# A hybrid layer of five token mixers: the attention's value products four key tiles at a time, its maxima transposed with 128 columns, its denominators after the next unit's products

## The chip, the cores and the metric

The kernel runs on one core of one Trainium2 chip. The metric is the device time of one execution in microseconds (us). Of the kernel before, three runs are given, and their median is the time that counts.

## What is computed

One layer over 2048 tokens of width 1024: a norm, one input projection to 4652 columns, five mixers of 256 columns each (spatial gate, forgetting attention "FoX", mLSTM, RWKV-7, attention to a memory of 256 rows), gates, and one output projection with the residual. The change touches the two attentions only:

```python
def forgetting_attention(q, k, v, f_logit, q_g, k_g):      # 4 heads of 64
    q = rms_norm(to_heads(q), q_g)
    k = rms_norm(to_heads(k), k_g)
    v = to_heads(v)
    big_f = jnp.cumsum(jax.nn.log_sigmoid(f_logit), axis=1)
    ...
        s = jnp.einsum("bthd,bshd->bhts", qb, k) * scale
        s = s + fb[..., :, None] - big_f[..., None, :]
        s = jnp.where(k_pos[None, :] <= q_pos[:, None], s, -jnp.inf)
        p = jax.nn.softmax(s, axis=-1)
        return jnp.einsum("bhts,bshd->bthd", p, v)
...
def memory_attention(q, mem_n, w_kv, q_g, k_g):            # 256 keys, no mask
    ...
    p = jax.nn.softmax(s, axis=-1)
    return jnp.einsum("bhtm,bmhd->bthd", p, v)
```

## The kernel before

The kernel goes through three phases of input projections and one of output projections. Each projection is done in three products of high and low parts on TensorE (L266, L288, L300, L314, L878). Beside them run "lanes": generators that issue a stage of other work at each `tick()`, which comes every few projection products. All engines take their instructions in the order in which this interleaving issues them.

The attentions are one lane, `fox`, with 1.815 steps to a tick (1.0 to a tick during the output projection). Their work is cut into 32 units of 512 queries of one head: 16 of FoX with 4, 8, 12 and 16 key tiles of 128 keys (`nkt`), and 16 of the memory with 2. The order is 15 units of FoX, 4 of the memory, the last of FoX, 12 of the memory. `Attention.run` (L931) takes a unit `n` through `average`, in `nkt + 3` steps, and meanwhile issues `load` and `maxima` of unit `n + 2` and `finish` of unit `n - 1`; the loops at L838, L844 and L848 call steps with no projection work between them.

- `load` (L978): loads keys and queries, rounds them to high parts and takes low parts. The tile `qb` (68 rows) holds the high parts of the queries and four more rows; two of those are set to one at L1010 in every unit.
- `maxima` (L1029): scores with queries on partitions (L1025, L1027), reduced by VectorE (L1039); the row maxima go to a tile `mm` of 4 columns per 128 queries (two constant ones from L1062, and a high and a low part by `split4`, L1018 and L1019), are transposed by four products against an identity matrix (L1067) and copied to the last rows of `qb` (L1068).
- `weights` (L1070): two or three products (L1080, L1082 for the mask, L1083) to one of two PSUM banks `p2`, and an exponential on ScalarE (L1085).
- `rest` (L1088): GpSimd adds the exponentials of all key tiles (L1097, L1099).
- `product` (L1101): the values weighted, two key tiles at a time. Even tiles go to the left 64 columns of the array, odd ones to the right 64, so a pair runs side by side. There is one PSUM bank `acc`, and the first product of the next unit waits until `finish` has read it.
- `finish` (L1123): copies one half of `acc` (L1137), adds the other (L1139), multiplies by the gate (L1141); the denominators are four products of 32 columns each (L1146), copied by ScalarE (L1148).
- `quotient` (L1151): a chain of DMAs through DRAM in ten stages, one at each call of `Attention.end`: denominators out (L1156), two stages later back in another shape (L1160), two later the reciprocal and out (L1163, L1164), two later in to 64 partitions (L1168), two later the product on VectorE (L1171), one later out to the gated branches (L1173). Each step of `run` calls `end` once; at its start, `finish` calls `end` again and again while more than one quotient is under way (L1131).

The output projection of 512 queries begins when the quotients of these queries are issued to the end (L848).

Of the kernel before, what the change touches and what calls it, by code (L numbers as in the profile page):

```python
# [35 lines left out]
# 256-column blocks of the input projection, by the first column of each  # L36
# [8 lines left out]
# narrow columns: (first column, width, first row of the transposed block)  # L45
NARROW = [(3340, 16, 0), (2564, 4, 16), (2568, 4, 20), (1536, 4, 24), (3868, 16, 32)]

# columns of the packed per-partition parameters
# [15 lines left out]
class Lane:  # L64
    """a queue of work that is emitted a stage at a time, between the parts of the projections"""
# [19 lines left out]
class Crowd:  # L85
    """short pieces of work that go on side by side, a stage at a time; a stage that has read a projection for the last
    time gives FREE"""
# [9 lines left out]
    def add(self, g, kind=None, most=2):  # L97
        """kind: what takes the same buffers, of which there are so many"""
        while sum(k == kind for _, k in self.all) >= most and kind:
            self.tick()  # L100
        if self.step(g):
            self.all.append((g, kind))
# [8 lines left out]
    def then(self, g):  # L111
        """g, behind all that is under way now"""
        wait = list(self.all)
        while any(x in self.all for x in wait):
            yield
        yield from g
# [3 lines left out]
def body(ctx: ExitStack, tc, x, xT, mem, memT, wp, wkv, wout, pv, wa, sguT, sgub, out, dbg=None):  # L120
# [26 lines left out]
    def rsqrt(t):  # L147
        """in place, of up to 16 positive columns: half of the exponent, negated, then Newton's steps to the last bit"""
# [8 lines left out]
    # parameters that stand behind a tanh, a doubled SiLU or a doubled GELU  # L157
# [47 lines left out]
    def load_w(parts, src, ncol=256):  # L205
        """hi and lo parts of a block of 256 columns, 2 row blocks to a tile"""
# [42 lines left out]
    def W(n):  # L249
        """the weights of this block; those of the next one are sent for"""  # L250
# [9 lines left out]
    def proj_T(wt, m, hts):  # L260
        """[128 columns, 512 tokens] of the projection"""
# [10 lines left out]
    def proj_narrow(wt, hts):  # L272
        """64 columns: the products of their hi parts above those of the lo parts"""
# [8 lines left out]
    def proj_T2(wt, hts, then=None):  # L282
        """both halves of a block at once: for the last use of the row blocks"""
# [10 lines left out]
    def proj_tok2(wt, hts, then=None, ntile=4):  # L294
        """all tokens at once"""
# [11 lines left out]
    def proj_tok(wt, hts, i):  # L307
        """[128 tokens, 256 columns] of the projection, twice: tokens i * 128 on and the next 128"""
# [11 lines left out]
    def split_h(hts, src_of, g, N):  # L320
        """hi and lo parts of (normalised x) * g, one tile for each of the 8 row blocks"""
# [16 lines left out]
    def send(*a):  # L338
        """the next row blocks are sent for"""
# [10 lines left out]
    def rstd(pool, tags, src, ntile):  # L350
        """1/rms of each token, tokens on partitions; tags: of the buffers for half of the columns of 128 tokens"""
# [20 lines left out]
    def rstd_rows(pool, tags, rb, src, ntile):  # L372
        """1/rms of each token, as a row over all partitions"""
# [4 lines left out]
    def over(ss, rb, ntile):  # L378
        """from tokens on partitions to a row over all partitions"""
# [5 lines left out]
    def gate(pt, o, then=lambda: None, free=FREE):  # L385
        """twice the SiLU"""
# [6 lines left out]
    def head_norm(pt, n, eps, pool=None):  # L393
        """1/rms over the 64 columns of each head; n columns on 128 tokens"""
# [13 lines left out]
    def qk_post(y, scale, d):  # L408
        """normalised over each head, scaled, transposed: to d"""
# [30 lines left out]
    def tok_cols(wt, hts, i, d):  # L440
        """tokens on partitions, to DRAM"""
# [10 lines left out]
    with ExitStack() as c1:  # L452
# [12 lines left out]
        def first(hts):  # L465
            """the first tokens: the norm is put to what comes out, so that the products need not wait for it"""
# [58 lines left out]
        for q in range(NQ):  # L525
# [8 lines left out]
            def shifted(pt, j, then):  # L534
                """token shift of a block of 128 columns"""
# [92 lines left out]
    def conv(pt, j, o):  # L628
        """causal convolution over 4 tokens, then twice the SiLU"""
# [13 lines left out]
    def group_B(q):  # L643
        """queries, keys, values and gates of FoX"""
# [11 lines left out]
    def group_M(q, then=None):  # L656
        """queries and gates of the attention to the memory"""
# [7 lines left out]
    for q in range(NQ):  # L665
# [32 lines left out]
    def gelu2(pt, o):  # L698
        """twice the tanh GELU"""
# [33 lines left out]
    # keys and values of the memory; its norm is put to what comes out  # L733
# [27 lines left out]
    for q in (NQ - 1, 0, 1, 2):  # L761
# [4 lines left out]
        if q == NQ - 1:  # L766
# [12 lines left out]
            # the first quarter of the attention to the memory goes before the last part of FoX  # L779
# [5 lines left out]
            # masked transposed weights and bias rows of the spatial gate  # L785
# [37 lines left out]
    def load_wo():  # L823
        """hi and lo parts of 128 rows of one half of the columns"""
# [22 lines left out]
    for q in range(NQ):  # L847
# [4 lines left out]
        def load_m(j):  # L852
            """256 tokens of the gated branches"""
# [34 lines left out]
class Attention:  # L888
    """what the attentions share"""
# [7 lines left out]
    def open(self):  # L897
# [8 lines left out]
        # 0 where the key may be seen, with keys on partitions, then with queries there  # L906
# [12 lines left out]
        self.minus = fp.tile([P, 1, 1], F32, bufs=1, name="minus")  # L919
        G.memset(self.minus, -1.0)  # L920
        self.two = fp.tile([P, 32], F32, bufs=1, name="two")
        G.memset(self.two, 2.0)

# [38 lines left out]
class Unit:  # L962
# [145 lines left out]
    def average(self):  # L1108
        self.acc = self.att.bank("acc")
        late, pair = deque(), []  # L1110
        for kt in range(self.nkt + 3):
# [4 lines left out]
            if kt > 2:  # L1116
                pair.append(late.popleft())
                if len(pair) == 2:
                    self.product(pair)
                    pair = []  # L1120
# [631 lines left out]
```

## Time and profile before

| | us |
|---|---|
| three runs | 1748.2, 1752.41, 1760.76 |
| median | 1752.41 |
| profiled execution, first to last instruction | 1753.3 |
| TensorE busy in it | 1654.2 |
| VectorE busy | 1197.5 |
| ScalarE busy | 880.9 |
| GpSimd busy | 302.8 |

PE is TensorE's products, PEld its weight loads, DVE VectorE, ACT ScalarE, POOL GpSimd, SP the queue that issues most DMAs. Matmul records overlap, as products are pipelined: what a product costs the engine is read from the start of one line to the start of the next. A product of plain f32 leaves two records, one of the rounded type (fp32r, as L266, L1067, L1080 and L1083) one. "Idle" in brackets is time in which the engine did nothing, and after the arrow is what ended it. The attentions' units lie between about 989 and 1602 us from the start of the span; the last 150 us are output projection alone.

### The profile page before, as it was taken

To read this page: it belongs to the slowest core of one execution; us is meant where nothing else is said; L and a number is where in the kernel's file an instruction comes from. 1 tells how busy PE (TensorE), PEld (TensorE's weight loads), DVE (VectorE), ACT (ScalarE), POOL (GpSimd) and SP (SyncE) were. 2 spreads that over 40 slices of the span, in tenths; PEclk is the share of its full clock that TensorE was granted. 3 is DMA by queue.
4 is the path that set the end of the run, shared out by engine and by line. 5 is a ranking of instruction groups with operands and counts; after the bars stand their busy time and mean duration, and the time that the engine had idled before them with its cause. 6 is when DMAs were issued, how large, how long until landed. Compare 5 with 4: busy or idle time off the path is not lost.

```text
span 1753.3 us, 31654 instructions
## 1 busy us (share of the span) xinstructions
PE 1654.2 (94%) x11306; PEld 1282.0 (73%) x11306; DVE 1197.5 (68%) x2990; ACT 880.9 (50%) x1895; POOL 302.8 (17%) x356
## 2 busy tenths in 40 slices
PE   8889999899999999999999899998999998899999
PEld 6667777787978888787888666756655665577887
DVE  7688684775978579587766986878576777642220
ACT  5566654544464545446455765565555657531110
POOL 5020000010101001010000244354444142000000
PEclk9999999899999999999999999999999999899999
DMA  6878554443544354344435554434324335754431
GB/s 207 259 236 245 179 173 101 137 118 94 144 130 122 104 149 124 85 123 129 119 88 167 148 152 112 109 95 121 85 78 111 106 77 162 184 142 122 129 125 59
DMA packets 200151, 234.36 MB, mean 134 GB/s; under 512 B 75016, under 2 KB 107336, under 8 KB 199992
## 3 DMA queue, kind: packets, MB, share of 16 engines
q1 hardware_dynamic: 185144, 218.69, 43.6%
q10 hardware_dynamic: 14848, 13.64, 2.6%
q8 instruction: 89, 1.46, 0.4%
q14 instruction: 70, 0.57, 0.1%
HBM read 180.44 MB, written 51.81 MB: 132 GB/s over the span
## 4 chain that ended last, share of the span: by engine, by line
PE 58%; DVE 18%; DMA 14%; ACT 6%; issue 4%; SPq 1%; POOL 0%; ACTq 0%; DVEq 0%; POOLq 0%
PE pj L266 12%; PE pj L878 12%; PE pj L314 11%; DMA wraw<-in_wp 4%; PE pj L288 3%; PE acc L1106 3%; DMA xr<-hbd 3%; DVE wt L224 2%; PE wk L1025 2%; DMA ao<-dn 2%; PE p L1080 2%; PE p L1083 1%; PE pj L300 1%; DMA xr<-in_xT 1%; DVE rq L153 1%
## 5 line engine op out<-in xcount | busy, mean ns | idle before, releaser
L266 PE MATMUL pj<-ht,wt 128*128 128x512 f32 x1632 | 427.6, 404 | 6.0 <-ACT ht L328 4.2
L266 PEld LDWEIGHTS pj<-ht,wt 128*128 128x128 f32 x1632 | 298.3, 190 | 83.8 <-issue 9.8
L314 PE MATMUL pj<-wt,ht 128*128 128x256 f32 x2400 | 337.3, 292 | 6.9 <-ACT ht L328 2.4
L314 PEld LDWEIGHTS pj<-wt,ht 128*128 128x128 f32 x2400 | 308.1, 195 | 24.6 <-issue 5.8
L224 DVE TENSOR_TENSOR wt<-wraw,wt 128x512 fp32r<-128x512 f32 (+1 forms) x312 | 220.3, 709 | 94.0 <-ACT wt L221 92.5
L221 ACT CAST wt<-wraw 128x512 fp32r<-128x512 f32 (+1 forms) x312 | 184.7, 600 | 148.8 <-DMA wraw<-in_wp 103.1
L878 PE MATMUL pj<-wo,mt 128*128 128x512 f32 x960 | 232.7, 399 | 2.5 <-ACT wo L829 2.3
L878 PEld LDWEIGHTS pj<-wo,mt 128*128 128x128 f32 x960 | 180.3, 190 | 53.7 <-issue 6.9
L1099 POOL TENSOR_TENSOR es<-es,pe 128x512 f32<-128x512 f32 (+3 forms) x128 | 155.2, 1212 | 107.9 <-ACT pe L1085 99.2
L288 PE MATMUL pj<-ht,wt 128*128 128x512 f32 x480 | 135.5, 421 | 13.3 <-ACT wt L221 12.4
L1085 ACT ACTIVATE pe<-p 128x512 f32<-128x512 f32 x192 | 100.7, 541 | 67.9 <-PE p L1083 65.4
L1039 DVE TENSOR_REDUCE mx<-wk 128x1 f32<-128x512 f32 (+3 forms) x192 | 112.5, 615 | 16.6 <-PE wk L1025 11.2
L288 PEld LDWEIGHTS pj<-ht,wt 128*128 128x128 f32 x480 | 91.2, 199 | 38.1 <-ACT wt L221 12.8
L1106 PE MATMUL acc<-pe,v 128*64 128x512 f32 (+3 forms) x384 | 106.9, 580 | 5.9 <-DVE at L1139 5.1
L1097 POOL TENSOR_TENSOR es<-pe 128x512 f32<-128x512 f32 (+1 forms) x32 | 43.3, 1353 | 249.3 <-ACT pe L1085 207.1
L329 DVE SCALAR_TENSOR_TENSOR ht<-xr,pvt,ht 128x512 fp32r<-128x512 f32 (+1 forms) x88 | 68.6, 786 | 24.8 <-ACT ht L328 24.1
L858 ACT CAST mt<-mr 128x256 fp32r<-128x256 f32 x80 | 31.9, 406 | 102.7 <-DVE xr L882 45.9
L1080 PE MATMUL p<-qa,kb 128*128 128x512 f32 x192 | 76.9, 400 | 6.7 <-ACT pe L1085 6.7
L328 ACT ACTIVATE ht<-xr,pvt 128x512 fp32r<-128x512 f32 (+1 forms) x88 | 61.0, 701 | 42.5 <-DMA xr<-hbd 26.7
L882 DVE TENSOR_TENSOR xr<-pj,xr 128x512 f32<-128x512 f32 x32 | 22.0, 688 | 85.6 <-PE pj L878 85.5
L1025 PEld LDWEIGHTS wk<-ka,qb 66*128 66x128 f32 x224 | 40.4, 191 | 49.5 <-issue 17.7
L1025 PE MATMUL wk<-ka,qb 66*128 66x512 f32 (+3 forms) x224 | 72.5, 378 | 4.2 <-DVE mx L1039 1.4
(332 smaller groups left out, 2471.5 us busy)
## 6 DMA issues: line engine op xcount, KB each, us to landing
wraw<-in_wp SPq DMA_DIRECT2D x288, 256.0 KB
xr<-hbd SPq DMA_DIRECT2D x56, 256.0 KB
mr<-mix SPq DMA_DIRECT2D x80, 128.0 KB
xr<-in_x SPq DMA_DIRECT2D x32, 256.0 KB
out<-xr ACTq DMA_DIRECT2D x32, 256.0 KB
xt<-in_x SPq DMA_DIRECT2D x24, 256.0 KB
xr<-in_xT SPq DMA_DIRECT2D x24, 256.0 KB
hbd<-xr SPq DMA_DIRECT2D x24, 256.0 KB
```

Of the source, the lines that this page charges most:

```text
L221: A.copy(wt[:, :, 0, :ncol], raw[:, :, :ncol])
L224: V.tensor_tensor(lo, raw[:, :, :ncol], wt[:, :, 0, :ncol].bitcast(F32), op=ALU.subtract)
L266: T.matmul(pt, wt[k // 2][:, k % 2, a, m * P:(m + 1) * P], hts[k][:, b, :], start=n == 0, stop=n == 3 * KT - 1)
L288: T.matmul(pts[m], wt[k // 2][:, k % 2, a, m * P:(m + 1) * P], hts[k][:, b, :], start=k + n == 0, stop=k == KT - 1 and n == 2)
L314: T.matmul(pt[:, ii * 256:ii * 256 + 256], hts[k][:, a, (i + ii) * P:(i + ii + 1) * P], wt[k // 2][:, k % 2, b, :], start=n == 0, stop=n = ...
L878: T.matmul(po, mts[i // 2, k][:, a, i % 2 * P:(i % 2 + 1) * P], wo[e * NK + k][:, b], start=n == 0, stop=n == 3 * NK - 1)
L1025: T.matmul(p1, self.qb[0:66, i * P:(i + 1) * P], self.k[kk][0][0:66, :w], start=True, stop=True, skip_group_check=diag)
L1039: V.tensor_reduce(*late.pop(), axis=AX.X, op=ALU.max)
L1080: T.matmul(p2[:, f:], kb[:, ks], self.qa[:, f:], start=True, stop=False)
L1085: A.activation(e[:, f:], p2[:, f:], AF.Exp)
L1099: G.tensor_tensor(self.sum[:, f:], self.sum[:, f:], e[:, f:], op=ALU.add)
L1106: self.att.nc.tensor.matmul(self.acc[64 * i:64 * i + 64, f:], self.v[:, kt], e[:, f:], start=kt < 2, stop=True, skip_group_check=True)
```

## The change

Five edits, all in `Attention` and `Unit`; in addition comments and docstrings of the whole file are dropped.

1. `product` takes four key tiles at a time (two in a unit of the memory), even ones left and odd ones right as before; the buffers of exponentials grow from 6 to 9.
2. `mm` has 128 columns per 128 queries, of which 64 to 67 are used and the others are zero; there are two such tiles, zeroed once. L1067's products thus have 128 columns instead of 4.
3. The two rows of ones in the three `qb` tiles and the two constant columns of `mm` are written once, in `open`, instead of in each unit.
4. The denominators are four products of 64 columns, on two halves of the array, instead of four of 32 on four quarters; they are not issued by `finish` but by the next unit's `product`, right behind its first group of value products. The last unit's are issued at once.
5. The copy of the denominators is 256 columns wide instead of 128, and the first DMA of `quotient` has another shape for it.

```diff
-        self.minus = fp.tile([P, 1, 1], F32, bufs=1, name="minus")
-        G.memset(self.minus, -1.0)
-        self.two = fp.tile([P, 32], F32, bufs=1, name="two")
+        self.two = fp.tile([P, 64], F32, bufs=1, name="two")
         G.memset(self.two, 2.0)
+        self.qbs, self.mms, self.count, self.late = [], [], 0, []
+        for i in range(3):
+            self.qbs.append(fp.tile([68, Q], F32R, bufs=1, name=f"qb{i}"))
+            A.copy(self.qbs[-1][64:66], self.ones[64:66].to_broadcast([2, Q]))
+        row = fp.tile([P, P], F32, bufs=1, name="row")
+        G.memset(row, 0.0)
+        G.memset(row[:, 64:66], -1.0)
+        for i in range(2):
+            self.mms.append(fp.tile([P, 4, P], F32R, bufs=1, name=f"mm{i}"))
+            for j in range(4):
+                A.copy(self.mms[-1][:, j], row)
...
-            flane.q.append(u.finish())
+            flane.q.append(u.finish(n + 1 == len(units)))
...
-        self.qb = fp.tile([68, Q], F32R, tag="qb", bufs=3, name="qb")
+        self.qb, self.mm = att.qbs[att.count % 3], att.mms[att.count % 2]
+        att.count += 1
         A.copy(self.qa, qr)
-        A.copy(self.qb[64:66], att.ones[64:66].to_broadcast([2, Q]))
...
-        mm = fp.tile([P, 4, 4], F32R, tag="mm", name="mm")
-        A.copy(mm[:, :, 0:2], att.minus.to_broadcast([P, 4, 2]))
-        self.split4(mx[:, :, 0], mm[:, :, 2:4])
+        mm = self.mm
+        self.split4(mx[:, :, 0], mm[:, :, 66:68])
         yield
         pm = att.bank()
         for i in range(4):
-            T.matmul(pm[0:4, i * P:(i + 1) * P], mm[:, i], att.identr, start=True, stop=True)
-        A.activation(self.qb[64:68], pm[0:4], AF.Copy, scale=-1.0)
+            T.matmul(pm[:, i * P:(i + 1) * P], mm[:, i], att.identr, start=True, stop=True)
+        A.activation(self.qb[64:68], pm[64:68], AF.Copy, scale=-1.0)
...
-        e = fp.tile([P, Q], F32, tag="pe", bufs=6, name="pe")
+        e = fp.tile([P, Q], F32, tag="pe", bufs=9, name="pe")
...
-        for i, (kt, f, e) in enumerate(pair):
+        for kt, f, e in pair:
+            i = kt % 2
             if kt == 1:
                 self.f = f
             self.att.nc.tensor.matmul(self.acc[64 * i:64 * i + 64, f:], self.v[:, kt], e[:, f:], start=kt < 2, stop=True, skip_group_check=True)
+        while self.att.late:
+            self.att.late.pop()()
...
-                if len(pair) == 2:
+                if len(pair) == min(4, self.nkt):
...
-    def finish(self):
+    def finish(self, last=False):
...
-        pd = att.bank()
-        for i in range(4):
-            T.matmul(pd[32 * i:32 * i + 32, 0:P], att.two, self.sum[:, i * P:(i + 1) * P], start=True, stop=True)
-        o = fp.tile([P, P], F32, tag="od", name="od")
-        A.copy(o, pd[:, 0:P])
-        att.tails.append(self.quotient(t, o))
+        def denominators():
+            pd = att.bank()
+            for i in range(4):
+                T.matmul(pd[64 * (i % 2):64 * (i % 2) + 64, i // 2 * P:(i // 2 + 1) * P], att.two, self.sum[:, i * P:(i + 1) * P], start=True, stop=True)
+            o = fp.tile([P, 2 * P], F32, tag="od", name="od")
+            A.copy(o, pd[:, 0:2 * P])
+            att.tails.append(self.quotient(t, o))
+        att.late.append(denominators)
+        if last:
+            att.late.pop()()
...
-        SY.dma_start(dn[0].rearrange("(i q) -> i q", q=P), od.rearrange("(i r) q -> i r q", r=32)[:, 0])
+        SY.dma_start(dn[0].rearrange("(b a q) -> a b q", a=2, q=P), od.rearrange("(a r) (b q) -> a r b q", r=64, q=P)[:, 0])
```

## Rows read from the trace of the kernel before

**Rows 1.** Busy time by stage: stretch, length, busy us of PE, PEld, DVE, ACT, POOL

```profile
990.00:1446.00 456.00, 427.34 (x2367) 291.46 (x2364) 342.01 (x640) 262.09 (x518) 190.29 (x154) 0.97 0.40 106
```

**Rows 2.** Chain that ended last, by line: 990 to 1446, then 1446 to 1530

```profile
by line: PE acc L1106 10.5%; PE pj L266 10.0%; PE pj L314 9.3%; PE wk L1025 6.8%; PE p L1080 5.3%; DMA xr<-hbd 5.3%; PE p L1083 4.9%; issue 3.8%; PE pj L288 3.7%; DVE rq L153 2.1%; DMA ao<-dn 2.0%; DVE wt L224 2.0%; DMA wraw<-in_wp 1.8%; DV
...
by line: DMA ao<-dn 16.3%; DMA wr<-in_wout 9.4%; issue 8.9%; DMA dn<-rc 7.8%; PE pj L266 5.2%; DMA mr<-mix 5.0%; DVE wo L830 4.6%; ACT pe L1085 3.3%; PE pj L878 3.2%; DMA mix<-mo 2.8%; DVE mt L859 2.8%; DVE qa L1013 2.3%; ACT qb L1012 2.2%;
```

**Rows 3.** Line L1106 alone: count and forms; its busy time in two stretches

```profile
L1106 PE MATMUL acc<-pe,v x384: 272/593/1117, 989.5 to 1592.0; 128*64 128x512 f32 x144, 128*64 128x384 f32 x16, 128*64 128x256 f32 x16, 128*64 128x128 f32 x16
...
990.00:1446.00 456.00, 89.25 (x335) 17.71 (x332) 0.97 0.40 106
1446.00:1530.00 84.00, 11.63 (x35) 2.05 (x32) 0.96 0.62 170
```

**Rows 4.** Timeline of TensorE: start us, us, line, form, count; around two pairs of values

```profile
1262.29 0.65 PE L1106 MATMUL acc<-pe,v 128*64 128x256 f32 x4
1262.87 1.69 PE L314 MATMUL pj<-wt,ht 128*128 128x256 f32 x12
...
1281.61 0.39 PE L1083 MATMUL p<-qb,ka 68*128 68x512 f32 x1
1281.93 1.08 PE L1106 MATMUL acc<-pe,v 128*64 128x512 f32 x4
1282.94 0.39 PE L1025 MATMUL wk<-ka,qb 66*128 66x256 f32 x1
1283.16 0.22 PE L1027 MATMUL wk<-mask,identr 128*128 128x128 f32 x1
```

**Rows 5.** The same view: the spatial gate's 16 products of 64 columns in a row

```profile
1025.71 1.97 PE L725 MATMUL wk<-sgw,gv 128*64 128x128 f32 x32
1027.61 0.51 PE L1080 MATMUL p<-qa,kb 128*128 128x512 f32 x1
```

**Rows 6.** The same view: the transposes of the maxima, and the denominators

```profile
1263.92 0.64 PE L314 MATMUL pj<-wt,ht 128*128 128x256 f32 x4
1264.40 0.40 PE L1067 MATMUL wk<-identr,mm 128*4 128x128 f32 x4
1264.64 0.44 PE L1080 MATMUL p<-qa,kb 128*128 128x512 f32 x1
1264.92 0.40 PE L1083 MATMUL p<-qb,ka 68*128 68x512 f32 x1
...
1269.19 0.39 PE L1083 MATMUL p<-qb,ka 68*128 68x512 f32 x1
1269.51 0.43 PE L1146 MATMUL wk<-es,two 128*32 128x128 f32 x8
1269.86 0.51 PE L1080 MATMUL p<-qa,kb 128*128 128x512 f32 x1
1270.21 0.40 PE L1083 MATMUL p<-qb,ka 68*128 68x512 f32 x1
```

**Rows 7.** The same view: products with 128-column weights and 128 columns streamed

```profile
1013.79 0.28 PE L1082 MATMUL p<-mask,identr 128*128 128x128 f32 x1
1013.90 0.28 PE L1083 MATMUL p<-qb,ka 68*128 68x128 f32 x1
```

**Rows 8.** Groups on ScalarE, 930 to 1620: the two constant copies

```profile
L1010 ACT CAST qb<-ones 2x512 fp32r<-2x512 f32 x32 | 19.7, 614 | 0.8
L1062 ACT CAST mm<-minus 128x8 fp32r<-128x8 f32 x32 | 6.3, 197 | 0.3
```

**Rows 9.** Chain that ended last, in order of time, 1440 to 1530: one of L1010's pieces

```profile
1459.29 0.61 ACT qb L1010
```

**Rows 10.** Timeline of VectorE and TensorE at the last FoX unit's start

```profile
1417.84 1.12 DVE L1171 TENSOR_TENSOR ao<-ao,at 64x512 f32<-64x512 f32 x1 [5.57 <-DMA ao<-dn]
...
1420.35 1.08 PE L1106 MATMUL acc<-pe,v 128*64 128x512 f32 x4 [2.52 <-DVE at L1139]
```

**Rows 11.** Timeline of ScalarE while the attention opens

```profile
943.77 0.62 ACT L221 CAST wt<-wraw 128x512 fp32r<-128x512 f32 x1 [2.63 <-DMA wraw<-in_wp]
```

## The prediction

> **What bounds the kernel now.** I read the stages first. In the stretch of the FoX units TensorE is busy 427 of 456 us, VectorE 342 and ScalarE 262 [rows 1]: on this view TensorE is the limit, and whatever is cut from it looks like time. The chain that ended last says less. There the products named add up to 50.5% (10.5 + 10.0 + 9.3 + 6.8 + 5.3 + 4.9 + 3.7), the rest being VectorE, DMAs and ScalarE [rows 2]. TensorE is nearly always busy, but at many moments it works off a backlog while what comes next waits for another engine. For the line that the change is mostly about I can say how often: L1106 has 10.5% of 456 us, 47.9 us, on the chain, out of 89.25 us that it is busy there [rows 2, 3]: 0.54. That is the share of a cut that I expect to see in the end, and I use it for all TensorE terms. In the stretch after it, where 12 units of the memory run beside the first output projection, the chain is one of DMA round trips: `ao<-dn` has 16.3% and `dn<-rc` 7.8% [rows 2], both of `quotient`.
>
> Last I read the timeline of TensorE from start to start. Four projection products of 256 columns take 1264.40 - 1263.92 = 0.48 us [rows 6]: 0.12 for 256 columns, 0.24 for 512. Against this measure the attention's small products can be priced.
>
> **Edit 1, four key tiles at a time.** A pair of 512 columns takes 1282.94 - 1281.93 = 1.01 us, one of 256 takes 1262.87 - 1262.29 = 0.58 [rows 4]. The difference, 0.43, is 256 columns; so 512 columns stream in 0.86, and 0.15 is fixed. The product before the pair takes 1281.93 - 1281.61 = 0.32 instead of 0.24, and the 256 columns after it 1283.16 - 1282.94 = 0.22 instead of 0.12 [rows 4]. One visit to the two halves of the array thus costs 0.15 + 0.08 + 0.10 = 0.33 us beyond its columns. Does a longer visit pay that once? The spatial gate has 16 such products in a row, 8 pairs of 128 columns, in 1027.61 - 1025.71 = 1.90 us [rows 5]; less 0.15 that is 0.22 for a pair of 128, the streaming rate (0.43 / 2). So yes. There are 192 value products [rows 3] (144 + 3 x 16): 160 of FoX in 80 pairs, 32 of the memory in 16. FoX goes to 40 groups, the memory keeps its pairs: 40 x 0.33 = 13.2 us less. A burst of four is some 1.9 us long; ScalarE has two score banks to work on meanwhile, so I cost the unevenness at nothing, and at one exponential's wait per group if that cover fails.
>
> **Edit 4, the denominators.** Now they cost 1269.51 - 1269.19 = 0.32 instead of 0.24 on the way in, 0.35 themselves and 1270.21 - 1269.86 = 0.35 instead of 0.24 on the way out [rows 6]: 0.54. Behind the value products, in the same halves, they are two more pairs of 128 columns, 2 x 0.22 = 0.44, with no way in or out. 32 x 0.10 = 3.2 us less. The wider copy on ScalarE has no waiter but the DMA.
>
> **Edit 2, the transposes.** Four products with 4-column weights take 1264.64 - 1264.40 = 0.24, the product before them is not lengthened (the 0.48 above ends there), and the next takes 0.28 instead of 0.24 [rows 6]: 0.28 in all. With 128 columns each product brings a full weight load. The nearest row is a mask product between two others of 128 columns: 1013.90 - 1013.79 = 0.11 [rows 7]. Four are 0.44: 0.16 more, 32 times, 5.1 us more. The bounds are 0.06 each (no more than streaming, a gain of 1.3 us) and 0.11.
>
> The Trainium skill's page "TensorEngine Tiling (Array Packing)", section "Tiling Modes", says under its key properties that changing the tiling mode drains the engine. By that rule a 4-column product would be a visit like the denominators', and edit 2 would save what I count as a cost; the sum would be some 6 us lower. The trace agrees for the 64- and 32-column products and shows no such wait ahead of the 4-column ones.
>
> TensorE in all: -13.2 - 3.2 + 5.1 = -11.3 us, of which 0.54, **-6.1**, should be seen.
>
> **Edit 3, constant rows.** 19.7 + 6.3 us leave ScalarE [rows 8]. It is busy 57% of the stretch, so most is off the path; on the chain L1010 stands three times between 1440 and 1530, at 0.61 or 0.62 [rows 9]: **-1.8**. The bounds are 0 and -26. In return `open` copies 8 squares and 3 pairs of rows; at no more than 0.61 each, 6.7 us at worst. ScalarE waits 2.63 us for weights soon after [rows 11] and the first scores come later still, so I take 0.
>
> **What moves.** A FoX unit's first value product comes at step 6 instead of 4. At the last FoX unit TensorE stood 2.52 us for VectorE's reading of the accumulator, because VectorE had waited 5.57 us for a `quotient` [rows 10]. Two more steps of other work are worth more than that: **-2.5** (bound 0).
>
> The denominators are issued three steps later in FoX and one step later in a unit of the memory, and the ten stages of `quotient` with them. In FoX there are steps enough. In the memory's units, of five steps, `finish` finds two quotients under way at every second unit and drives them on at once. By the code it drives three stages now; with the later start it drives four, and the fourth is decisive: L1168's load and the product L1171 that needs it are then issued with no step between them, and the reciprocal's DMAs also lose a step. VectorE stands for that, and behind it its reductions, the parts of `wo` and `mt` and the sums that free the output banks; SP stands at L1173 with the next loads behind it. One step is 84 us over 35 / 4 pairs and five steps to each, 1.9 us [rows 3]. In the stretch 1446 to 1530 there are four such places: 0 to 7.6 us; later TensorE has output products to do. The lost step may pass beside waits that are there anyhow. I take half: **+3.8**.
>
> **Sum:** -6.1 - 1.8 - 2.5 + 3.8 = -6.6. From 1753.3 that is 1746.7, and as the profiled execution is 0.9 above the median of the runs, 1745.8: **1746 us**. Its own range is 1740 to 1752, from the bounds of the tail (0, +7.6) and of the transposes.
>
> **Rivals.** (a) TensorE, at 94% [rows 1], passes on every cut: -11.3 - 1.8 - 2.5 and no loss in the tail, 1753.3 - 15.6 - 0.9 = 1737. For it: busy time. Against: half of the chain is elsewhere. Chance 0.15. (b) The cut becomes idle time before VectorE and DMA, the tail takes the rest: 1752. For it: VectorE's 75% and the DMAs of the chain [rows 1, 2]. Chance 0.18. (c) Slower: the late `quotient` holds VectorE at all eight forced places, and the last FoX unit waits as now: -6.1 - 1.8 + 8 x 1.9 = +7.3, 1760. It decides from the point where VectorE stands longer than TensorE's work in hand; at the last FoX unit that was some 3 us (5.57 - 2.52) [rows 10]. For it: the chain of 1446 to 1530. Against: only the earlier half of those units is short of projection work. Chance 0.14. (d) The 4-column products change the array's mode unseen, and their way in and out goes away as for the denominators (0.08 + 0.11), with none of the 0.16: 32 x 0.35 x 0.54 = 6 us below the forecast, 1740. Against: nothing is lengthened ahead of them [rows 6]. Chance 0.05. That is the page's rule above. The forecast has the remaining 0.48.
>
> About 1% (17.5 us) is what a measurement of this kernel can tell from no change. Below 1734.9 lies about a third of (a) and a little of the others' spread, 0.10 in all; above 1769.9 only the far side of (c), 0.08. Within 1%: 0.82. The range reaches to (a) and (c): 1735 to 1761.
>
> **What would show it.** Groups of eight L1106 records on the timeline, some 1.9 us for 512 columns, and 40 fewer ways in and out; L1146 right behind them with no gap; L1067's four at 0.44 instead of 0.24. No wait of L1106 for L1139 at the last FoX unit. L1171 waiting longer for `ao<-dn` among the memory's units. TensorE's busy time in the FoX stretch should fall by more than the span does. I am wrong if groups of four still show a wait between the pairs, if the transposes stay at 0.24, or if the stretch before 1446 shrinks by the full cut.

## The result and the profile after

The changed kernel takes 1765.8 us in the median of 11 runs, the kernel before 1752.41 in 11 runs beside them: ratio 1.0074, 95% interval 1.0054 to 1.0093. It is 13 us slower; the forecast was 1746, with 1761 as the upper end of the range. The ratios in this text are those of the runs on record, and they differ from the quotient of the two medians by up to 0.14%. The profiled execution has a span of 1762.7 us (before 1753.3). TensorE is busy 1656.4 us of it, VectorE 1198.6, ScalarE 862.4: ScalarE's work fell by 18.5 us, the others' hardly moved.

The prices of single instructions came out as forecast. The first lines below are the timeline of TensorE after the change (start us, us, line, form, count), to be held against [rows 4] and [rows 6]. L1116 is the product of the values (L1106 before), L1076 the transposes (L1067), L1160 the denominators (L1146).

```profile
1149.17 0.33 PE L1092 MATMUL p<-qb,ka 68*128 68x256 f32 x1
1149.43 1.94 PE L1116 MATMUL acc<-pe,v 128*64 128x512 f32 x8
1151.30 0.45 PE L1035 MATMUL wk<-ka,qb 66*128 66x384 f32 x1
1151.58 0.23 PE L1037 MATMUL wk<-mask,identr 128*128 128x128 f32 x1
...
1270.04 0.56 PE L1076 MATMUL wk<-identr,mm 128*128 128x128 f32 x4
1270.43 0.45 PE L1089 MATMUL p<-qa,kb 128*128 128x512 f32 x1
1270.72 0.40 PE L1092 MATMUL p<-qb,ka 68*128 68x512 f32 x1
...
1278.14 1.94 PE L1116 MATMUL acc<-pe,v 128*64 128x512 f32 x8
1279.91 0.61 PE L1160 MATMUL wk<-es,two 128*64 128x128 f32 x8
1280.45 0.50 PE L1035 MATMUL wk<-ka,qb 66*128 66x512 f32 x1
```

A group of four takes 1151.30 - 1149.43 = 1.87 us, which is 2 x 0.86 + 0.15: one way in and out, as forecast. The transposes take 0.39 and lengthen the product behind them from 0.24 to 0.29: 0.44 in all, as forecast. The denominators follow the values with no gap. Both together take 1280.45 - 1278.14 = 2.31, which is 0.44 more than a group by itself, as forecast.

By stage (length, busy us of PE, PEld, DVE, ACT, POOL, then PE's granted clock, DMA share, GB/s), the changed kernel:

```profile
990.00:1446.00 456.00, 420.53 (x2372) 310.83 (x2372) 342.52 (x643) 250.29 (x480) 192.19 (x154) 0.97 0.38 106
...
1446.00:1486.00 40.00, 38.44 (x208) 26.94 (x207) 22.86 (x43) 19.21 (x37) 7.99 (x6) 1.00 0.27 64
1486.00:1530.00 44.00, 35.71 (x137) 23.22 (x138) 30.27 (x59) 24.83 (x51) 5.41 (x4) 0.81 0.70 192
```

and the kernel before in the last two of these stretches:

```profile
1446.00:1486.00 40.00, 36.74 (x215) 24.26 (x212) 28.82 (x56) 27.89 (x60) 8.89 (x7) 1.00 0.53 153
1486.00:1530.00 44.00, 36.23 (x172) 21.75 (x171) 33.30 (x65) 27.43 (x55) 4.96 (x4) 0.93 0.70 185
```

In the FoX stretch TensorE works 6.8 us less than in [rows 1]. Behind it something else has changed: from 1446 to 1486 us the DMA queues carry 64 GB/s instead of 153, and from 1486 on TensorE gets a mean granted clock of 0.81 instead of 0.93 (its two levels are 1.2 and 2.4 GHz) and finishes 137 records instead of 172. The timeline of SP shows which transfers are missing (start us, us, line, out<-in, count). Before:

```profile
1446.50 1.35 SPq L828 DMA_DIRECT2D wr<-in_wout  x3
1447.90 0.43 SPq L856 DMA_DIRECT2D mr<-mix  x1
...
1449.71 1.06 SPq L856 DMA_DIRECT2D mr<-mix  x2
```

After:

```profile
1489.63 1.35 SPq L828 DMA_DIRECT2D wr<-in_wout  x3
...
1496.08 0.94 SPq L828 DMA_DIRECT2D wr<-in_wout  x2
1497.06 0.42 SPq L856 DMA_DIRECT2D mr<-mix  x1
```

The first rows of the output weights (`wr`) and of the mixed values (`mr`) start 43 and 49 us later. They belong to the pool `op` of the output projection (opened at L841). It takes the place of FoX's keys and reaches below them, so the size of the attention's own pool `fp` decides where it lies: in the program's allocation, `op` started at byte 113,888 of a partition before and starts at 102,144 now. `sp2`, the pool of the last spatial-gate blocks, holds its rows up to byte 112,384 until their last use near 1486 us. Before, 1,504 bytes were free between them; the change added 11,744 bytes to `fp` (three more buffers of exponentials 6,144, two wide `mm` 4,096, the rest `row`, `od`, `two` and less of the old constants), and now the two overlap.

This shows as another order and not as a wait in the queue: from 1440 to 1500 us of the changed kernel SP waits 0.5 us in all at L828. In the program as it is built, the first `wr` load is the 974th of SP's 1198 transfers before. It is the 1006th in the changed kernel, behind the last store of the spatial gate's blocks (`mix<-mo`, the 1004th). So the order on the engines is not that of the interleaving alone, as the text ahead of the prediction has it: it depends on which memory is free as well, and the order on TensorE, VectorE and ScalarE changes with that on SP.

Where the difference arises is read best from one and the same projection product in both traces. The table gives how much later (+) or earlier (-) than in the kernel before it starts, in us, at the product that starts there at the time above; single traces stand between -6.2 and +3.5 us at 990 already, so the columns are to be compared with each other. The column 1486 is the first output product. A trace is one execution: b_pad's is the slowest of its 12 runs (1771.18 us, their median 1763.04), a_ox's the fastest of its 12 (1752.9, median 1759.44).

| kernel | 990 | 1160 | 1430 | 1446 | 1486 | 1500 | 1600 |
|---|---|---|---|---|---|---|---|
| after | -0.1 | +7.4 | -4.4 | -1.3 | +11.2 | +16.5 | +8.6 |
| b_four | -5.2 | -7.6 | -19.2 | -12.0 | -3.9 | +2.4 | -0.7 |
| b_pad | +3.5 | +3.0 | +3.0 | +3.6 | +11.5 | +17.8 | +15.6 |
| b_four_ox | -2.9 | -4.5 | -11.9 | -5.7 | -6.1 | -3.6 | -1.6 |
| four_again | -6.2 | -5.5 | -16.2 | -9.5 | -9.0 | -6.9 | -2.2 |
| f_late | -4.5 | +4.4 | -9.5 | -7.0 | -3.9 | -5.0 | -6.7 |
| a_ox | -4.0 | +4.7 | -6.4 | -3.3 | +0.1 | -2.0 | -3.0 |
| b_ox | -1.0 | -1.6 | -5.5 | -4.7 | -3.3 | -0.8 | -3.4 |
| b_wr7 | -2.5 | -1.2 | -3.1 | -2.4 | -3.2 | -5.9 | -7.4 |

The changed kernel leads by 4.4 us at 1430, by 1.3 at 1446, and lags by 16.5 at 1500. A part of that lag is order: from the product at 1446 to the first output product TensorE works off 255 records now and 219 before, and to the product at 1600 it is 697 in both. From 1446 to 1600 the changed kernel loses 9.9 us. The same work in the kernel before, and then in the changed kernel:

```profile
1446.36:1600.10 153.74, 141.72 (x697) 96.33 (x697) 92.00 (x179) 76.14 (x161) 19.02 (x14) 0.97 0.57 157
1445.05:1608.70 163.65, 151.02 (x697) 107.09 (x697) 91.27 (x179) 70.89 (x143) 18.58 (x14) 0.95 0.53 148
```

TensorE's idle time hardly grows (12.6 us instead of 12.0). It is busy 9.3 us longer over as many records, in part at the lower clock.

### The profile page after: what moved, and what is told of

The parts are those of the page before. It is cut to its first block, busy times and chain, and to the rows that moved or that the text cites. A ratio compares the mean times of both kernels' runs of the same rounds, so it can differ in the third digit from the quotient of the medians.

```text
span 1762.7 us, 31639 instructions
## 1 busy us (share of the span) xinstructions
PE 1656.4 (94%) x11306; PEld 1310.9 (74%) x11306; DVE 1198.6 (68%) x2990; ACT 862.4 (49%) x1842; POOL 304.0 (17%) x357
## 4 chain that ended last, share of the span: by engine, by line
PE 56%; DVE 20%; DMA 12%; ACT 5%; issue 4%; POOL 1%; SPq 0%; ACTq 0%; DVEq 0%; POOLq 0%
PE pj L266 12%; PE pj L878 12%; PE pj L314 10%; DMA wraw<-in_wp 3%; DVE wt L224 3%; PE acc L1116 3%; PE pj L288 2%; DVE mx L1049 2%; PE pj L300 2%; DMA ao<-dn 2%; PE wk L1035 2%; DVE rq L153 2%; DMA xr<-hbd 1%; DVE ht L329 1%; PE p L1089 1%
## 5 line engine op out<-in xcount | busy, mean ns | idle before, releaser
L314 PE MATMUL pj<-wt,ht 128*128 128x256 f32 x2400 | 331.0, 288 | 5.5 <-DVE gz L389 1.5
L314 PEld LDWEIGHTS pj<-wt,ht 128*128 128x128 f32 x2400 | 304.0, 192 | 19.6 <-issue 2.4
L1116 PE MATMUL acc<-pe,v 128*64 128x512 f32 (+3 forms) x384 | 105.6, 578 | 6.0 <-DVE at L1151 5.4
L1106 POOL TENSOR_TENSOR es<-pe 128x512 f32<-128x512 f32 (+1 forms) x32 | 43.3, 1354 | 268.1 <-ACT pe L1094 198.2
L1089 PE MATMUL p<-qa,kb 128*128 128x512 f32 x192 | 76.2, 398 | 12.2 <-ACT pe L1094 12.2
L329 DVE SCALAR_TENSOR_TENSOR ht<-xr,pvt,ht 128x512 fp32r<-128x512 f32 (+1 forms) x88 | 71.6, 820 | 21.6 <-ACT ht L328 21.3
L858 ACT CAST mt<-mr 128x256 fp32r<-128x256 f32 x80 | 31.8, 406 | 109.3 <-DVE xr L882 47.1
L1092 PE MATMUL p<-qb,ka 68*128 68x512 f32 x192 | 75.2, 395 | 1.0 <-ACT qb L1077 1.0
```

The lines of the kernel that those rows point to most:

```text
L314: T.matmul(pt[:, ii * 256:ii * 256 + 256], hts[k][:, a, (i + ii) * P:(i + ii + 1) * P], wt[k // 2][:, k % 2, b, :], start=n == 0, stop=n = ...
L1089: T.matmul(p2[:, f:], kb[:, ks], self.qa[:, f:], start=True, stop=False)
L1116: self.att.nc.tensor.matmul(self.acc[64 * i:64 * i + 64, f:], self.v[:, kt], e[:, f:], start=kt < 2, stop=True, skip_group_check=True)
```

## The experiments

All ratios are against the kernel before on the same chip.

**First: which edit?** The rivals were the late denominators (1), the bursts of four (2) and the wide transposes (3). Four kernels: the changed kernel with the denominators issued in `finish` again (a_now), with 4-column transposes (a_narrow), with pairs (a_pairs), and the kernel before with groups of four and nine buffers of exponentials alone (b_four).

```diff
a_now     -        att.late.append(denominators)
          +        denominators()
a_narrow  -  mms.append(fp.tile([P, 4, P], F32R, ...))
          +  mms.append(fp.tile([P, 4, 4], F32R, ...))
a_pairs   -  if len(pair) == min(4, self.nkt):
          +  if len(pair) == 2:
b_four    -  if len(pair) == 2:
          +  if len(pair) == min(4, self.nkt):
          -  e = fp.tile([P, Q], F32, tag="pe", bufs=6, name="pe")
          +  e = fp.tile([P, Q], F32, tag="pe", bufs=9, name="pe")
```

> The changed kernel, but the denominators are issued by finish, at the step where they stood before (still 64 columns wide). Theory 1 (the late start of quotient holds VectorE in its order, and TensorE behind it): the loss is gone, 1742 to 1750 us, and the gain of the value groups shows. Theory 2 (bursts of four value products delay the scores and maxima): no change from the changed kernel, 1762 to 1768. Theory 3 (the wide transposes): no change either.

> The changed kernel, but the maxima are transposed with 4 columns as before (constant columns still written once). Theory 1: 0.54 of 5 us back, 1762 to 1765. Theory 2: the same. Theory 3 (the wider weight loads stand where VectorE's maxima already hold TensorE, so that they count more than in full): 1753 to 1758.

> The changed kernel, but values weighted two key tiles at a time; the denominators then come behind the first pair, at step 4 instead of 6 in FoX. Theory 1: the delay in FoX is one step instead of three, so a part of the loss goes, but 13 us of TensorE time come back, 1760 to 1768. Theory 2: 1752 to 1757, no slower than before.

> The kernel before with the values four key tiles at a time and nothing else. Theory 1: 7 us faster than before (0.54 of 13.2 us), 1743 to 1748. Theory 2: slower than before, 1756 to 1765. If TensorE's time were the limit throughout: 1739.

Measured: a_now 1.0089 (1.0055 to 1.0123), a_narrow 1.0066 (1.0041 to 1.0090), a_pairs 1.0125 (1.0095 to 1.0155), b_four 1.0015 (0.9988 to 1.0042). No undone edit brings the time back, so none of the three theories alone is the cause; groups of four are a gain inside the change (a_pairs is the slowest of the four). b_four wins 14.0 us between 990 and 1430 and loses 21.6 between 1430 and 1500, 7.2 of them before 1446, where no output weight is needed yet. All four have grown `fp`, and all load their first `wr` late (b_four at 1476.10, a_pairs at 1495.67).

**Second: the memory.** b_pad is the kernel before with an unused buffer. In b_four_ox and a_ox the four buffers of x, 8 KB, are taken out of `op` into a pool `ox` of their own below it, so that the rest of `op` stands above byte 112,384 again (115,936 and 112,384). b_four_const_ox adds edit 3 to b_four_ox.

```diff
b_pad   +        pad = fp.tile([P, 2936], F32, bufs=1, name="pad")
        +        G.memset(pad[:, 0:4], 0.0)
*_ox    +    ox = att.c4.enter_context(tc.tile_pool(name="ox", bufs=4, side="right"))
        -                xr = op.tile([P, 512], F32, tag="xr", bufs=4, name="xr")
        +                xr = ox.tile([P, 512], F32, tag="xr", bufs=4, name="xr")
a_ox    -        raw = op.tile([P, 512], F32, tag="wr", bufs=3, name="wr")
        +        raw = op.tile([P, 512], F32, tag="wr", bufs=2, name="wr")
```

> The kernel before with nothing added but an unused buffer of 11,744 bytes per partition in the attention's pool, as much as the change added to it. Theory S (space): the pool of the output projection then starts at byte 102,144, which the pool of the last blocks' raw rows still holds up to byte 112,384; its first loads, which start at 1446.5 us in the kernel before, start at about 1485 to 1492 us, TensorE finds too little work between 1486 and 1515 us, and the time is 8 to 14 us above the kernel before, ratio 1.005 to 1.008. Rival R (the loss comes from the order of the attention's own work): memory that nobody uses changes nothing, ratio 0.998 to 1.002.

> The kernel before with groups of four and three more buffers of exponentials, and with the buffers of x (8 KB) taken out of the output projection's pool into one of their own below it, so that the loads of weights and of mix stand above byte 112,384 again. Theory S: the first loads start before 1450 us again and the 13 us that four key tiles won by 1430 us are kept: about 1740 us, ratio 0.990 to 0.995. Rival R: as with four key tiles alone, 1754 us, ratio 0.999 to 1.003.

> The changed kernel with the same move of the buffers of x, and two buffers of output weights' raw rows in place of three. Theory S: the first loads start before 1450 us again, the time falls from 1765.8 by 10 to 13 us to about 1753 to 1756 us, ratio 0.999 to 1.002. Rival R: it stays at 1762 to 1768 us, ratio 1.005 to 1.009.

> As the kernel with groups of four and the moved buffers of x, with the constant rows written once (three lasting query tiles taken in turn, two lasting tiles of maxima, four columns wide). Of the 13 us that groups of four won by 1430 us the changed kernel kept about 4. If the lasting tiles are what cost it that, TensorE is 6 to 10 us behind the kernel with groups of four at 1160 us and the time is about 1747 us; if they only save their copies, it is within 2 us of that kernel, about 1738 to 1741 us.

Measured: b_pad 1.0050 (1.0024 to 1.0076), b_four_ox 0.9965 (0.9943 to 0.9987), a_ox 1.0028 (1.0006 to 1.0049), b_four_const_ox 0.9983 (0.9957 to 1.0009). b_pad computes nothing new and is 0.5% slower, 9 us. On TensorE, VectorE, ScalarE and SP it has the instructions of the kernel before, but in another order from the first `wr` load on, which is SP's 1006th transfer as in the changed kernel. Its trace shows the same picture as the changed kernel's, by stage:

```profile
1446.00:1486.00 40.00, 38.16 (x214) 24.48 (x214) 25.48 (x50) 24.29 (x48) 9.45 (x9) 1.00 0.21 57
1486.00:1530.00 44.00, 34.25 (x146) 19.68 (x141) 31.27 (x59) 27.77 (x57) 5.78 (x5) 0.81 0.69 192
```

and on SP's timeline its first output weights:

```profile
1491.41 0.54 SPq L828 DMA_DIRECT2D wr<-in_wout  x1
```

In a_ox, which has all the edits and one buffer of `wr` less, the loads are early again (the first `wr` is the 974th transfer) and the clock is back:

```profile
1446.00:1486.00 40.00, 36.02 (x203) 24.67 (x201) 30.15 (x61) 25.40 (x55) 9.72 (x7) 0.98 0.45 134
1486.00:1530.00 44.00, 42.62 (x196) 30.05 (x197) 30.44 (x57) 21.88 (x43) 3.84 (x3) 0.94 0.67 188
```

```profile
1443.71 1.01 SPq L828 DMA_DIRECT2D wr<-in_wout  x2
1444.77 1.37 SPq L857 DMA_DIRECT2D mr<-mix  x3
```

So the memory by itself costs 0.50% (0.24 to 0.76%): 9 us, with 4 and 13 as the ends. The changed kernel less a_ox (1.0074 less 1.0028) gives 0.46%, but these two were measured at different times, and a_ox has the smaller `wr`. With its loads early a_ox is still no faster than the kernel before. What the late loads cost and what the changed order costs is not separated: the two come together in all of these kernels.

Part of it is clock: at 0.81 in place of 0.93, 44 us hold (0.93 - 0.81) x 44 = 5.3 us less of full speed. In the changed kernel TensorE, with gaps of 8.3 us in these 44 (7.8 before), has the low level for 17.0 us between 1490 and 1517; the kernel before has it for 3.4 us there and again from 1527 on. In the five traces in which the first `wr` comes after 1487 us (after, a_now, a_narrow, a_pairs, b_pad) the clock of this stretch is 0.77 to 0.81, in the fifteen others 0.85 to 1.00.

**Third: what is left.** f_late is b_four_ox with edit 4; f_wide is a_ox without edit 4; b_ox is the kernel before with the pool `ox` alone. f_mix was meant to keep pairs in the memory's units (`4 if self.fox else 2`). But such a unit has two key tiles, so `min(4, self.nkt)` is two there already: f_mix is b_four_ox once more, and its expectation rests on my misreading.

> As b_four_ox, with groups of four for the FoX units alone; the units against the memory keep pairs. Of the 12 us that b_four_ox had won over the kernel before at 1430 us, 1.6 were left at 1580 us. If the late products of the memory units are what gives it back (their quotients come later, and the output projection waits for them), most of it is kept: 1740 to 1744 us, ratio 0.991 to 0.995. If the stretch behind 1486 us is bound by the round trips of the quotients and the loads whatever the groups are, it is as b_four_ox, 1747 to 1751 us, ratio 0.995 to 0.998.

> As b_four_ox, with the change's edit 4 alone: denominators 64 columns wide, behind the next unit's first values. If the late quotients are what the changed kernel loses beyond its memory (VectorE standing for ao while TensorE waits for the maxima, as at 1159 to 1169 us), 5 to 8 us above b_four_ox: 1754 to 1757 us, ratio 1.000 to 1.003, and TensorE's lag against b_four_ox grows between 1100 and 1200 us. If not, within 2 us of b_four_ox, or 2 us below it by the prices of its instructions.

> The changed kernel in the layout of a_ox, with its edit 4 undone: groups of four, constant rows once, maxima transposed at full width, denominators of 32 columns in the unit's own finish. If the full width costs what its instructions cost, 32 times 0.16 us or 5 us, of which half shows: 1751 to 1754 us, ratio 0.999 to 1.001. If edit 4 is the cause of the 10 us between a_ox and b_four_ox, it is no more than that; if the full width is the cause, it is as a_ox, 1757 to 1760 us, ratio 1.002 to 1.005.

> The kernel before with nothing but the buffers of x in a pool of their own. Its loads of weights and of mix stood free of other pools already, so the move should change nothing: 1751 to 1755 us, ratio 0.998 to 1.002. If the move by itself is what b_four_ox wins, it is at 1747 to 1750 us, ratio 0.995 to 0.998.

Measured: f_mix 1.0002 (0.9983 to 1.0021), f_late 0.9996 (0.9979 to 1.0013), f_wide 0.9993 (0.9974 to 1.0012), b_ox 1.0017 (0.9996 to 1.0037). f_mix and b_four_ox, the same program on two chips, are 0.37% apart, more than either interval says, so a price for edit 4 had to be measured on one chip. What its traces do show is a jam in a FoX unit: at its start VectorE waits for a late quotient, and TensorE then for the maxima. The changed kernel's timelines of VectorE and TensorE:

```profile
1154.24 0.17 DVE L1181 RECIPROCAL rc<-rc 128x4 f32<-128x4 f32 x1
...
1159.17 0.68 DVE L1189 TENSOR_TENSOR ao<-ao,at 64x512 f32<-64x512 f32 x1 [3.99 <-DMA ao<-dn]
```

```profile
1163.51 1.08 PE L1076 MATMUL wk<-identr,mm 128*128 128x128 f32 x4 [5.38 <-DVE mm L1029]
```

In f_wide, without edit 4, the reciprocal comes at 1144.69, its quotient has arrived by 1151.02, and there is no wait. late_slack gives the last multiplication of a FoX unit's quotient two more steps (four_slack the same without edit 4); late_again and four_again are f_late and b_four_ox on the same chip.

```diff
         yield
         yield
+        if self.fox:
+            yield
+            yield
         V.tensor_tensor(o, o, t, op=ALU.mult)
```

> As f_late, with the last multiplication of a FoX unit's quotient two steps of the schedule later, so that VectorE comes to it behind its transfer. If the jam at 1152 to 1163 us (VectorE 4.0 us at ao, then TensorE 5.4 us at the maxima) is what the late denominators cost, the jam is gone (under 1 us of either wait there), TensorE is 4 to 6 us ahead of f_late at 1160 us, and the time is 3 to 5 us below f_late measured beside it, as four_again. If it is not, the time is within 2 us of late_again.

> f_late once more, beside four_again on one chip, since their two ratios come from different chips. If edit 4 costs what the two ratios say, 3 to 6 us above four_again; if the difference was the chips', within 2 us of it.

> b_four_ox once more: 0.9965 of the kernel before again, 1744 to 1747 us where the kernel before takes 1751 us; or within 2 us of it, if that ratio was the chip's.

> b_four_ox with the same two steps for the last multiplication of a FoX unit's quotient. VectorE waited 10.1 us for ao between 990 and 1446 us; if TensorE pays for a part of that, 2 to 4 us below four_again; if VectorE's waits are hidden there, within 2 us of it.

Measured: late_slack 1.0018 (0.9998 to 1.0039), late_again 1.0004 (0.9987 to 1.0021), four_again 1.0005 (0.9985 to 1.0026), four_slack 0.9985 (0.9965 to 1.0005). Side by side, edit 4 costs nothing that can be measured. late_slack did not test the jam, as the multiplication still stands close behind the reciprocal in the built program, and VectorE's wait stayed:

```profile
1155.67 0.17 DVE L1173 RECIPROCAL rc<-rc 128x4 f32<-128x4 f32 x1
...
1160.61 0.68 DVE L1184 TENSOR_TENSOR ao<-ao,at 64x512 f32<-64x512 f32 x1 [4.01 <-DMA ao<-dn]
```

But a_now tests it: with the denominators in `finish` the jam isn't there (TensorE waits 1.7 us in all between 1130 and 1180), and a_now is as slow as the changed kernel.

The table shows besides that a lead at 1430 is worth nothing at the end: b_four_ox and four_again win 9.0 and 10.0 us from 990 to 1430 and give back 10.3 and 14.0 by 1600, 6.2 and 6.7 of them by 1446. That first part goes at the end of the last FoX unit. There, in all traces with groups of four, TensorE waits 1.8 to 4.7 us for an exponential, and in before, b_pad, b_ox and b_wr7 it does not. ScalarE had stood for a row of the input weights. In four_again:

```profile
1427.46 0.60 PE L1081 MATMUL p<-qa,kb 128*128 128x384 f32 x1 [4.69 <-ACT pe L1086]
1424.32 0.62 ACT L221 CAST wt<-wraw 128x512 fp32r<-128x512 f32 x1 [6.71 <-DMA wraw<-in_wp]
```

The chain that ended last runs there from 1409.9 to 1420.3 us over VectorE, and then over that load (4.03 us).

**Fourth: what bounds the end.** b_wr7 is b_ox with seven buffers for `wr` instead of three, with FoX untouched; four_wr6 is four_slack with six of them and seven buffers of exponentials. Both start `op` at byte 113,888.

```diff
b_wr7    -        raw = op.tile([P, 512], F32, tag="wr", bufs=3, name="wr")
         +        raw = op.tile([P, 512], F32, tag="wr", bufs=7, name="wr")
```

> As b_ox, with seven buffers of output weights' raw rows in place of three (8 KB more; the pool starts at byte 113,888, still free of the last blocks' rows, which end at 112,384). In the kernel before ScalarE waited 11.0 us for these rows between 1480 and 1530 us, behind the three that were loaded at 1446.5 us. If the loads of the output weights are what bounds the stretch behind 1486 us, four more of them in the buffers beforehand win 3 to 6 us: ratio 0.996 to 0.998 of the kernel before. If the stretch is bound by the round trips of the quotients, nothing: ratio 0.999 to 1.002.

> As four_slack, with seven buffers of exponentials in place of nine and six of output weights' raw rows in place of three (the pool starts at byte 113,888). Groups of four lead the kernel before by 9 to 16 us at 1430 us and by 2 to 9 us at 1600 us. If the loads of the output weights take the difference, more of the lead is kept: ratio 0.992 to 0.996, 1737 to 1744 us. If they do not, it is as four_slack, ratio 0.997 to 1.000; if seven buffers of exponentials are too few for groups of four, TensorE waits for pe and leads by less than 6 us at 1430 us.

Measured: b_wr7 0.9951 (0.9930 to 0.9972), 1744.39 us; four_wr6 0.9959 (0.9938 to 0.9980), 1745.27 us. Both beat both kernels. The next lines show the waits of ScalarE from 1440 to 1530 us (waited for: us in total, times, longest), before and in b_wr7, and SP's first loads in b_wr7:

```profile
ACT wo L829 <- DMA wr<-in_wout: 11.0, 8, 3.9
```

```profile
ACT wo L829 <- DMA wr<-in_wout: 6.4, 7, 1.9
```

```profile
1445.25 1.96 SPq L828 DMA_DIRECT2D wr<-in_wout  x4
...
1447.80 1.53 SPq L828 DMA_DIRECT2D wr<-in_wout  x3
```

Seven loads stand ready instead of three, ScalarE's wait falls by 4.6 us, and between 1486 and 1500 the kernel gains 2.7 us where b_ox loses 2.5. That the loads of the output weights bound that stretch is what the times say, 0.9951 against 1.0017 for b_ox; ScalarE's wait by itself does not measure it, as it is 5.0 us in the changed kernel, 5.3 in b_pad and 12.2 in a_ox, and the order of the instructions in b_wr7 changes with its buffers too. four_wr6 with its long lead (19.1 us at 1430) is no faster than b_wr7 without one: what groups of four win is not kept even then. The leads of all these traces at 1600 us do not follow those at 1430.

## Why the prediction was wrong

**The step that failed is one that isn't there.** The prediction costs what the edits take from the engines and adds, part by part, and nothing for the memory that they add. The diff shows `pe` from 6 to 9 buffers and `mm` from 4 to 128 columns, and I read them as instructions alone. The chain from 1446 to 1530 had `DMA wr<-in_wout` at 9.4% and `DMA mr<-mix` at 5.0% [rows 2]: these loads were on the path, and my text names the quotient's items of that row alone. A step from `fp`'s size to where `op` lies would have found it. The cost is 9 us (4 to 13), about half of the 20 us between forecast and measurement. The forecast gain of 6.6 us is not there either: with the loads early a_ox stands at 1.0028 and f_wide, without edit 4, at 0.9993. That term failed by its size, the share of 0.54. Some 4 us stay open.

**Edit 1** was right in its price (1.87 us for a group, the way in and out once). The Trainium skill, "TensorEngine Tiling (Array Packing)", section "Tiling Modes", says that a change of the tiling mode drains TensorE; the trace agrees for the 64-column products, with 0.28 instead of 0.18 us for the 384 columns behind the group, and no run here bears on how the drain itself works. Of the 13.2 us b_four, four_again and b_four_ox have 14.0, 10.0 and 9.0 at 1430, but 6.8, 3.3 and 2.8 at 1446, where the FoX stretch ends (f_mix has the most there, 7.4): 0.2 to 0.6 of the cut. The prediction put the unevenness of groups at nothing; TensorE's waits for `pe` from 990 to 1446 are 6.4 us before and 13.3, 10.7 and 14.0 in these three.

**The share of 0.54** is near the upper end of that, and far above what is left at the last instruction. It was read inside one stretch and used for the whole kernel. The same kernel with groups of four and its loads in place measures 0.9965, 1.0002 and 1.0005: nearly all is given back behind 1430. That is rival (b), to which I gave 0.18. Its condition, idle time before VectorE and DMA, is what the last FoX unit shows in four_again; for the stretch behind, b_wr7 speaks for the loads.

**Edit 2** cost its 0.44 against 0.28 for each of 32 units; it was a cost and not the saving of rival (d). **Edit 3** took ScalarE's copies as said (18.5 us less busy time, with the additions of `open`), and its -1.8 is not visible: b_four_const_ox 0.9983 lies between the results of b_four_ox. **Edit 4** has the forecast price, 0.44 against 0.54, and its 3.2 us are not seen either: late_again and four_again are even.

**What moves.** The last FoX unit's wait of 2.52 us for `at` [rows 10] is gone, as forecast: from 1400 to 1450 us TensorE waits for nothing but `pe`. But that wait, 2.7 us in all, stands in its place, so the -2.5 was not won. The tail was wrong: VectorE waits 16.8 us for `ao<-dn` from 1446 to 1620, before 17.2, so +3.8 was not there. Rival (c)'s mechanism, VectorE held by a late quotient, does occur, in FoX at 1159 and not among the memory's units; its end result of 1760 comes near the measured time for another reason.

**Left open.** a_ox stands at 1.0028 (1.0006 to 1.0049) and f_wide at 0.9993, while late_again beside four_again shows no price of edit 4. One kernel on different chips spreads by 0.4%, so the last 0.2 to 0.3% of the changed kernel's 0.74% may be that or a joint effect. Nor is it known why a_pairs is 0.75% above b_pad, with the same memory. That b_pad's cost comes from where the pools lie is shown, as nothing else was changed; that it is the late loads, and not the changed order beside them, is argued from its trace and from a_ox.

## What to carry to other kernels

A buffer count is an edit of its own: work out where every pool that opens later will lie, which live pool it will then overlap, and which loads come later for that; here 11,744 bytes where 1,504 were free cost 0.5%. Then look at the built order, as the order in the code does not show it. Eight KB given to the loads of the next stage won 0.49% (0.28 to 0.70); the whole change was forecast to win 0.38%. Before cutting the busiest engine's work, read what bounds the work behind it: a lead that arrives at loads not yet there is not a gain.

## What the runs showed of the hardware

The spread between runs of one kernel is mostly granted clock: in 35 runs of the kernel before (those beside b_pad) the span varies with a standard deviation of 5.3 us, and by 3.0 once (1 - clock) x span, 43.8 us in the mean, is taken off each. In b_pad's 12 runs 47.1 us are lost to the clock by the same product, so 3.3 of the 9.6 us between the means are clock. In b_pad's profiled execution the work from the product at 1446 to the one at 1600 has 17.7 us of TensorE's idle time at a clock of 0.93, in the kernel before 12.0 at 0.97: there the loss is of both kinds, idle time and the lower level.

```profile
1449.99:1615.70 165.71, 148.01 (x697) 99.04 (x697) 93.60 (x179) 76.74 (x161) 18.64 (x14) 0.93 0.53 146
```
